# Decay levels of a gated recurrence on 32-column groups of TensorE, with two reorderings on VectorE

## The chip, the cores and the metric

The kernel runs on one core of a Trainium2 chip. The metric is the time of one execution on the device, in microseconds (us). Before the change it is 1099.34 us, the median of 3 runs (1099.16 to 1099.45). The profiled execution took 1100.05 us.

## The reference, cut to what matters

Two layers, each a chain of a feed-forward block, a mixer, a cross attention and another feed-forward block on 256 tokens of width 1024, all in float32. The change touches the recurrence inside the mixer and the softmax inside the cross attention.

```python
# hgrn2, per chunk of 64 tokens, 4 heads of 128 channels
b = jnp.cumsum(lb_, axis=2)                       # lb_ = log of the forget gate
diff = b[:, :, :, None, :] - b[:, :, None, :, :]
decay = jnp.exp(jnp.where(mask[:, :, None], diff, -jnp.inf))
attn = jnp.einsum('bhtd,bhsd,bhtsd->bhts', qb, kb, decay)
o = (jnp.einsum('bhts,bhsv->bhtv', attn, vb)
     + jnp.einsum('bhtd,bhdv->bhtv', qb * jnp.exp(b), state))
...
# cross_attn: 4 heads of 256 channels, 256 memory tokens
sc = jnp.einsum('bshd,bmhd->bhsm', q, k).astype(jnp.float32) * (CA_HEAD_DIM ** -0.5)
p = jax.nn.softmax(sc, axis=-1).astype(v.dtype)
o = jnp.einsum('bhsm,bmhd->bshd', p, v).reshape(bsz, s, D_MODEL)
```

## The kernel before

Every large matrix product is made of three products of split operands: a tile is cut into a high part in the f32r format (`split`, L60, a ScalarE copy at L61) and the rest (a VectorE subtraction at L62). Weights arrive through three `raw` buffers on the SyncE queue, are split into eight `whi` and eight `wlo` buffers, and are consumed by `product` (L106). So each of TensorE, VectorE and ScalarE has a steady load through the whole program.

The mixer (`mixer`, L586) computes the 256x256 decay-weighted products of `q` and `k` as a tree. Tokens are held as two blocks (`NT`) of 128, the second one reversed. The diagonal is one product `k` by `q` per head and block, with the identity picked out of it (L690, L691). Then come seven levels, `LEVELS = (1, 2, 4, 8, 16, 32, 64)`. In each, ScalarE gathers `kc`, the half blocks of `k` of that width (L701, `blocks`), TensorE multiplies `kc` by the other half blocks of `q` for all four heads (L713), VectorE scales `k` and `q` by the decay of a level (L729, L732), and it copies the entries of the level into `AT` under a mask (L739, `copy_predicated`, twice). At L713 all 128 columns of `kc` of a head stand on TensorE against 128 columns of `q`, although level `c` uses only the squares of width `c` beside the diagonal.

```python
for hh in range(HEADS):
    nc.tensor.matmul(
        o[:, hh], kc[:, hh, :],
        view(qf, hh * P + c, (other - c, 2), (2 * c, a), (1, c)),
        start=True, stop=True,
    )
```

TensorE's order in this part is the order of the code (`manual_schedule`, L671). Between the levels stand other products of the mixer (`products_of_others`, L710): one or two of them ahead of each level, so that VectorE and ScalarE can prepare the next level meanwhile. Behind the levels, `recurrence` (L761) multiplies `AT` by the values. The other engines' queues are ordered by a scheduler that goes by the order of the code and by what is ready.

The attention (`attention`, L854) takes four heads. `weights` (L876) makes the scores of a head, their maximum (L885), the exponentials (L892) and the division (L900), and sends the result through four transfers that deal it out (L904). `turned` (L907) transposes the dealt tile on VectorE (L909) and splits it. `mixed` (L921) multiplies it by the values. The scores of heads 2 and 3 are made while the second half of the values is made (`values`, L938 to L946), after heads 0 and 1 have been turned.

`small_parameters` (L214) loads parameters at the start, and its `later` (L252) works on them on VectorE; `later` is called in the first feed-forward block (L540 to L542).

Of the kernel before, what the change touches and what calls it, by code (L numbers as in the profile page):

```python
# [17 lines left out]
P = 128  # L18
# [4 lines left out]
NT = SEQ // P  # L23
NK = DM // P
HEADS = 4
# [4 lines left out]
LEVELS = (1, 2, 4, 8, 16, 32, 64)  # L30
# [16 lines left out]
def model(ctx: ExitStack, tc: tile.TileContext, t: dict, out: bass.AP):  # L47
    nc = tc.nc
# [5 lines left out]
    def acc(shape=(P, 2, SEQ), tag="acc"):  # L54
        return ps.tile(list(shape), F32, tag=tag, name=tag)


    loads, normed = [], []

    def split(hi, lo, src):  # L60
        nc.scalar.copy(hi, src)  # L61
        nc.vector.tensor_tensor(lo, src, hi.bitcast(F32), op=ALU.subtract)  # L62

# [115 lines left out]
    def load_memory(mp, behind):  # L179
# [25 lines left out]
    wpool = cst.tile([P, DEPTH, 2, P], F32, name="wpool")  # L205
    masks = cst.tile([P, 1024], U8, name="masks")[:, 0 : NT * len(LEVELS) * 64].rearrange(
        "p (b n c) -> p b n c", b=NT, c=64
    )
    nc.gpsimd.memset(nhalf, -0.5)
# [4 lines left out]
    def small_parameters(op):  # L214
# [12 lines left out]

        mf = op.tile([P, NT, len(LEVELS), 64], F32, name="mf", bufs=1)
        nc.gpsimd.memset(mf, 1.0)
        for b in range(NT):  # L230
            for n, c in enumerate(LEVELS):
# [9 lines left out]
        made = nc.gpsimd.tensor_copy(masks, mf)  # L241

# [128 lines left out]
    def ffn(l, name, n, pend=None, last=False, early=None):  # L371
        gate, up, down = (t[f"{name}_{x}"][l] for x in ("gate", "up", "down"))
        with tc.tile_pool(name="ffn", bufs=2, reuse_waits="tile") as fp:
# [155 lines left out]
            for c, (c0, ncol) in enumerate(chunks):  # L529
# [56 lines left out]
    def mixer(l, fill):  # L586
        w_in = t["w_in"][l]
        with tc.tile_pool(name="mix", bufs=1, reuse_waits="tile") as mp:
# [13 lines left out]
            v = mp.tile([P, NT, 512], F32, name="v")  # L602
            AT = mp.tile([P, NT, HEADS, P], F32, name="AT")
            AX_ = mp.tile([P, HEADS, P], F32, name="AX_")

# [79 lines left out]

            other = HEADS * P
            for b in range(NT):
                o = acc((P, HEADS, P), "dn")
                for hh in range(HEADS):
                    nc.tensor.matmul(o[:, hh, :], k[:, b, hh, :], q[:, b, hh, :], start=True, stop=True)  # L690
                nc.vector.tensor_tensor(  # L691
                    AT[:, b], o, idn[:, None, :].to_broadcast([P, HEADS, P]), op=ALU.mult
                )
            nc.vector.tensor_tensor(q, q, f, op=ALU.mult)
# [3 lines left out]
            def blocks(c):  # L698
# [6 lines left out]
                return kc  # L705

            kc = blocks(1)
            for n, c in enumerate(LEVELS):
                a = 64 // c
                products_of_others((1, 2, 1, 2, 1, 2, 2)[n])  # L710
                o = acc((P, HEADS, NT, 64), "dn")
                for hh in range(HEADS):
                    nc.tensor.matmul(  # L713
                        o[:, hh], kc[:, hh, :],
                        view(qf, hh * P + c, (other - c, 2), (2 * c, a), (1, c)),
                        start=True, stop=True,
                    )
                na, tb = HEADS * a, other // c
# [14 lines left out]
                if c < 64:  # L733
# [3 lines left out]
                    tot = nt[:, :]  # L737
                for b in range(NT):
                    nc.vector.copy_predicated(  # L739
                        AT[:, b].rearrange("p h (a w c) -> p h a w c", w=2, c=c)[:, :, :, 1 - b, :],  # L740
                        masks[:, b, n, :].rearrange("p (a c) -> p a c", c=c)[:, None].to_broadcast(
                            [P, HEADS, a, c]
                        ),
                        o[:, :, b].rearrange("p h (a c) -> p h a c", c=c),
                    )
            w_gate = load(w_in, 0, NK, 2304, 512)
# [14 lines left out]
            def recurrence(i):  # L761
# [6 lines left out]
                ss = sm.tile([P, HEADS], F32, tag="ss", name="ss")  # L768
                jk = mp.tile([P, P], F32, tag="jk", name="jk", bufs=2)
                for hh in range(HEADS):  # L770
# [83 lines left out]
    def attention(l, pend):  # L854
        scale = (DM // HEADS) ** -0.5
        with tc.tile_pool(name="att", bufs=1, reuse_waits="tile") as ap:
# [3 lines left out]
            vl = ap.tile([P, NT, DM], F32R, name="vl")  # L860
            pr = [None] * HEADS

# [13 lines left out]
            def weights(hh):  # L876
# [21 lines left out]
                for i in range(NT):  # L898
                    v = e.rearrange("p (q i j) -> p i q j", i=2, j=32)[:, i]
                    nc.vector.tensor_scalar_mul(v, v, s[:, i : i + 1])  # L900

                x = ap.tile([P, 4, 4, 32], F32, tag="dealt", name="dealt", bufs=2)
                for a in range(4):
# [17 lines left out]
            def mixed(hh, pT):  # L921
                o = acc()
                for d in range(2):
# [73 lines left out]
```

## Time and profile before

| | before |
|---|---|
| median of 3 runs | 1099.34 us |
| profiled execution | 1100.05 us |
| span in the profile | 1098.3 us |
| outside the span | 1.75 us |
| mean granted TensorE clock | 0.998 |

A line of a time-ordered view has the start and the length in us, the engine, the line of the code, the operation with what it writes and reads, and how many were merged ("x8"). A line of the groups has busy time and the mean duration in ns. One float32 matmul shows as two records, on PE and on PEld (the load of the columns that stand still). The length of a PE record is a latency, and records overlap, so what a matmul costs is read from the distance of two starts.

### The profile page before, as it was taken

The page shows a single profiled execution, that of the slowest core. Times are in us where ns is not written, and L with a number is a line of the kernel's source. Part 1 is how long each engine was busy: PE and PEld are TensorE (multiplying, and loading weights), DVE is VectorE, ACT ScalarE, POOL GpSimd, SP SyncE. Part 2 cuts the span into 40 slices and gives each one's busy share as a digit, 9 for nine tenths or more (in the row PEclk, how much of TensorE's full clock was granted, in tenths as well). Part 3 has the DMA queues.
Part 4 walks back from the last instruction along what each step waited for, and adds up shares of the span by engine and source line. Part 5 has one row for each costly group of instructions (what it writes and reads, how often), then busy time and mean ns, then how long its engine had stood idle before and what let it go on. Part 6 is the DMA issues. An engine that isn't in the chain of part 4 may idle for free.

```text
span 1098.3 us, 14694 instructions
## 1 busy us (share of the span) xinstructions
PE 1086.8 (99%) x5619; PEld 964.8 (88%) x5619; DVE 848.2 (77%) x1101; ACT 565.3 (51%) x767; POOL 61.2 (6%) x112
## 2 busy tenths in 40 slices
PE   9999999999999999999999999999999999999997
PEld 7888888999899888888888888899998988888886
DVE  6678678998989777666687655798989888766665
ACT  6466454665556455444455445456564654544450
POOL 9500000000000000000000000000000000000000
PEclk9999999999999999999999999999999999999999
DMA  9987664745485496766478676656446665876751
GB/s 319 303 278 234 212 215 160 255 156 173 160 265 190 134 301 216 231 216 222 154 264 265 219 217 211 224 171 213 161 131 229 237 201 166 259 243 213 215 169 39
DMA packets 122662, 231.79 MB, mean 211 GB/s; under 512 B 6304, under 2 KB 45504, under 8 KB 117472
## 3 DMA queue, kind: packets, MB, share of 16 engines
q1 hardware_dynamic: 120800, 228.48, 64.2%
q0 software_dynamic: 1216, 1.20, 0.4%
q10 hardware_dynamic: 576, 1.18, 0.3%
q8 instruction: 44, 0.72, 0.3%
q14 instruction: 26, 0.21, 0.1%
HBM read 216.15 MB, written 1.05 MB: 198 GB/s over the span
## 4 chain that ended last, share of the span: by engine, by line
PE 93%; DVE 4%; issue 1%; ACT 1%; DMA 0%; DVEq 0%; ACTq 0%
PE acc L106 61%; PE dn L106 28%; PE acc L170 1%; PE dn L713 1%; DVE square L909 1%; DVE wlo L62 1%; ACT e L892 0%; DVE qTl L62 0%; DMA h<-in_x_dram 0%; PE dn L767 0%; PE dn L690 0%; DVE mx L885 0%; DVE xT L62 0%; ACT L892 0%; DVE vl L62 0%
## 5 line engine op out<-in xcount | busy, mean ns | idle before, releaser
L62 DVE TENSOR_TENSOR wlo<-raw,whi 128x1024 fp32r<-128x1024 f32 (+1 forms) x396 | 473.8, 1213 | 177.9 <-ACT whi L61 168.6
L61 ACT CAST whi<-raw 128x1024 fp32r<-128x1024 f32 (+1 forms) x396 | 402.5, 1041 | 336.5 <-PE dn L106 139.9
L106 PE MATMUL acc<-whi,xT 128*128 128x512 f32 x1312 | 395.0, 379 | 0.0
L106 PEld LDWEIGHTS acc<-whi,xT 128*128 128x128 f32 x1312 | 247.8, 189 | 35.0
L106 PE MATMUL acc<-wlo,xT 128*128 128x512 f32 x656 | 248.6, 379 | 0.0
L106 PE MATMUL acc<-xT,whi 128*128 128x512 f32 x576 | 141.8, 382 | 0.0
L106 PEld LDWEIGHTS acc<-wlo,xT 128*128 128x128 f32 x656 | 124.0, 189 | 17.5
L106 PE MATMUL dn<-whi,ah 128*128 128x512 f32 x346 | 131.5, 380 | 0.0
L106 PE MATMUL dn<-wlo,ah 128*128 128x512 f32 x346 | 131.1, 379 | 0.0
L106 PE MATMUL dn<-whi,al 128*128 128x512 f32 x346 | 131.1, 379 | 0.0
L106 PEld LDWEIGHTS acc<-xT,whi 128*128 128x128 f32 x576 | 104.2, 190 | 11.2
L106 PE MATMUL dn<-whi,xT 128*128 128x512 f32 x288 | 89.0, 383 | 0.0
L106 PEld LDWEIGHTS acc<-xT,wlo 128*128 128x128 f32 x576 | 75.5, 191 | 3.9
L106 PE MATMUL acc<-xT,wlo 128*128 128x256 f32 x576 | 75.9, 275 | 0.0
L106 PEld LDWEIGHTS dn<-whi,al 128*128 128x128 f32 x346 | 65.4, 189 | 9.2
L106 PEld LDWEIGHTS dn<-wlo,ah 128*128 128x128 f32 x346 | 65.4, 189 | 9.2
L106 PEld LDWEIGHTS dn<-whi,ah 128*128 128x128 f32 x346 | 65.4, 189 | 9.2
L413 DVE STREAM_TRANSPOSE square<-dealt 128x512 f32<-128x512 f32 x40 | 63.3, 1650 | 1.8 <-DMA dealt<-sg 1.8
L322 POOL TENSOR_TENSOR rs<-rs,nhalf 128x1 f32<-128x1 f32 x16 | 14.9, 933 | 857.6 <-DVE rs L321 857.6
L106 PEld LDWEIGHTS dn<-whi,xT 128*128 128x128 f32 x288 | 54.5, 190 | 8.5 <-DVE xT L62 1.1
L106 PE MATMUL dn<-wlo,xT 128*128 128x512 f32 x144 | 54.8, 381 | 0.0
L315 DVE SCALAR_TENSOR_TENSOR h<-h,dn 128x512 f32<-128x512 f32 x31 | 21.2, 683 | 30.2 <-PE dn L106 30.2
(198 smaller groups left out, 996.7 us busy)
## 6 DMA issues: line engine op xcount, KB each, us to landing
raw<-in_ffn_up_dram SPq DMA_DIRECT2D x44, 1024.0 KB, 5.1
raw<-in_ffn_down_dram SPq DMA_DIRECT2D x44, 1024.0 KB, 5.2
raw<-in_ffn_gate_dram SPq DMA_DIRECT2D x42, 1024.0 KB, 5.1
raw<-in_w_in_dram SPq DMA_DIRECT2D x24, 1024.0 KB, 5.1
dealt<-sg SPq DMA_DIRECT2D x80, 128.0 KB, 3.2
raw<-in_ca_k_dram SPq DMA_DIRECT2D x8, 1024.0 KB, 5.0
raw<-in_w_out_dram SPq DMA_DIRECT2D x8, 1024.0 KB, 5.0
raw<-in_ca_v_dram SPq DMA_DIRECT2D x8, 1024.0 KB, 5.8
```

The costliest lines, as they stand in the source:

```text
L61: nc.scalar.copy(hi, src)
L62: nc.vector.tensor_tensor(lo, src, hi.bitcast(F32), op=ALU.subtract)
L106: nc.tensor.matmul(o, w, x, start=start, stop=stop)
L170: nc.tensor.transpose(pt[:, k, :], src[:, (4 * j + k) * P : (4 * j + k + 1) * P], unit)
L315: nc.vector.scalar_tensor_tensor(v, v, ALPHA / scale, sums(y[i][n]), op0=ALU.mult, op1=ALU.add)
L322: nc.gpsimd.tensor_tensor(rs, rs, nhalf[:, 0:1], op=ALU.pow)
L413: nc.vector.transpose(d.rearrange("p k (i b) -> p b k i", b=4), x[:, :, i, :].rearrange("p b (j k) -> p b k j", k=4))
L713: nc.tensor.matmul(o[:, hh], kc[:, hh, :], view(qf, hh * P + c, (other - c, 2), (2 * c, a), (1, c)), start=True, stop=True,)
L909: nc.vector.transpose(pt.rearrange("p m (i r b) -> p b (m i) r", i=2, b=4), pr[hh])
```

## The change

Diagonal and levels: for every head the 128 columns of `k` or `kc` are cut into four groups of 32, and each group is multiplied by the 32 columns of `q` that it needs (64 in level 64), into the 32 partitions of the output that belong to the group. The result is gathered in `square`, 32 wide, by masks 16 wide, in the levels below 32. In levels 32 and 64 ScalarE copies the result into `AT`, which GpSimd has set to zero; `square` is copied into `AT` at level 32.

```diff
-            for b in range(NT):
-                o = acc((P, HEADS, P), "dn")
                 for hh in range(HEADS):
-                    nc.tensor.matmul(o[:, hh, :], k[:, b, hh, :], q[:, b, hh, :], start=True, stop=True)
-                nc.vector.tensor_tensor(
-                    AT[:, b], o, idn[:, None, :].to_broadcast([P, HEADS, P]), op=ALU.mult
-                )
+                    for g in groups:
+                        nc.tensor.matmul(o[g, b, hh, :], k[:, b, hh, g], q[:, b, hh, g], start=True, stop=True)
+            nc.vector.tensor_tensor(
+                square, o, idc[:, None, None, :].to_broadcast([P, NT, HEADS, 32]), op=ALU.mult
+            )
...
-                o = acc((P, HEADS, NT, 64), "dn")
+                o = acc((P, HEADS, max(c, 32)), "dn")
                 for hh in range(HEADS):
-                    nc.tensor.matmul(
-                        o[:, hh], kc[:, hh, :],
-                        view(qf, hh * P + c, (other - c, 2), (2 * c, a), (1, c)),
-                        start=True, stop=True,
-                    )
+                    for j, g in enumerate(groups):
+                        if c < 32:
+                            x = view(qf, hh * P + 32 * j + c, (other - c, 2), (2 * c, 16 // c), (1, c))
+                        else:
+                            x = q[:, j * 32 // c % 2, hh, later(j, c)]
+                        nc.tensor.matmul(o[g, hh, :], kc[:, hh, g], x, start=True, stop=True)
...
+                else:
+                    if c == 32:
+                        for g in groups:
+                            nc.scalar.copy(AT[g, :, :, g], square[g])
+                    for at in range(0, P, c):
+                        g = slice(at, at + c)
+                        nc.scalar.copy(AT[g, at // c % 2, :, later(at // 32, c)], o[g])
```

Attention: the transfers of a head move out of `weights` into `deal`, and the scores and softmax of heads 2 and 3 are written ahead of the turning of heads 0 and 1.

```diff
-            query(1, lambda: (weights(0), weights(1)))
+            query(1, lambda: (weights(0), deal(0), weights(1), deal(1)))
...
-                    2: lambda: (pT.extend((turned(0), turned(1))), weights(2), weights(3)),
+                    2: lambda: (weights(2), weights(3), pT.extend((turned(0), turned(1))), deal(2), deal(3)),
```

Parameters: `later` is issued behind the latest subtraction of a split.

```diff
                 if c == 2:
-                    for f in rest:
-                        f()
+                    with tc.issue_after(lows[-1].ins):
+                        for f in rest:
+                            f()
```

On TensorE's queue, at the diagonal and the first level of a mixer, the order before and now (x4 counts matmuls merged into a row; the last two numbers are output partitions and moving columns):

```order
-L690 MATMUL dn<-q,k 128x128 x8
...
-L713 MATMUL dn<-q,kc 128x128 x4
+L701 MATMUL dn<-q,k 32x32 x32
...
+L736 MATMUL dn<-q,kc 32x32 x16
 L106 MATMUL acc<-xT,whi 128x512 x7
```

The products between stay as they were; each set of 4 or 8 matmuls has become one of 16 or 32 of a quarter of the width, and in the last level the moving width is 64.

On VectorE's queue in the first attention, before (mx_3227 is of head 2, mx_3255 of head 3, square_3202 of head 0, square_3208 of head 1):

```order
L909 STREAM_TRANSPOSE square_3202<-dealt_3095 128x4x128
L885 TENSOR_REDUCE mx_3227<-dn_3214 128x2
L885 TENSOR_REDUCE mx_3255<-dn_3242 128x2
L62 TENSOR_TENSOR pTl_3205<-square_3202,pTh_3204 128x512
L886 TENSOR_SCALAR mx_3227<-mx_3227 128x2
L886 TENSOR_SCALAR mx_3255<-mx_3255 128x2
L909 STREAM_TRANSPOSE square_3208<-dealt_3123 128x4x128
L897 RECIPROCAL sum_3231<-sum_3231 128x2
L900 TENSOR_SCALAR e_3230<-e_3230,sum_3231 128x8x32 x2
L62 TENSOR_TENSOR pTl_3211<-square_3208,pTh_3210 128x512
L897 RECIPROCAL sum_3259<-sum_3259 128x2
L900 TENSOR_SCALAR e_3258<-e_3258,sum_3259 128x8x32 x2
```

The same place in the changed kernel (mx_3326 is of head 2, mx_3349 of head 3, square_3359 of head 0, square_3365 of head 1):

```order
L913 TENSOR_REDUCE mx_3326<-dn_3313 128x2
L941 STREAM_TRANSPOSE square_3359<-dealt_3206 128x4x128
L914 TENSOR_SCALAR mx_3326<-mx_3326 128x2
L913 TENSOR_REDUCE mx_3349<-dn_3336 128x2
L62 TENSOR_TENSOR pTl_3362<-square_3359,pTh_3361 128x512
L914 TENSOR_SCALAR mx_3349<-mx_3349 128x2
L941 STREAM_TRANSPOSE square_3365<-dealt_3234 128x4x128
L925 RECIPROCAL sum_3330<-sum_3330 128x2
L928 TENSOR_SCALAR e_3329<-e_3329,sum_3330 128x8x32 x2
L925 RECIPROCAL sum_3353<-sum_3353 128x2
L928 TENSOR_SCALAR e_3352<-e_3352,sum_3353 128x8x32 x2
L62 TENSOR_TENSOR pTl_3368<-square_3365,pTh_3367 128x512
```

The maximum of head 2 moved ahead of the first transposition, and the division of head 3 ahead of the last split; the operations are the same.

More of the change, by code (lines that the diff above doesn't have):

```diff
@@ L240, in small_parameters @@
                 )
-        made = nc.gpsimd.tensor_copy(masks, mf)
+        for j in range(4):
+            g = slice(32 * j, 32 * j + 32)
+            nc.gpsimd.tensor_copy(idc[g], idn[g, g])
+            made = nc.gpsimd.tensor_copy(masks[g], mf[g, :, :, 16 * j : 16 * j + 16])
         cnt = op.tile([P, 2, PAD], F32, name="cnt", bufs=1)
@@ L737, in mixer @@
                     tot = nt[:, :]
-                for b in range(NT):
[L739 to L745, printed above, removed]
+                if c < 32:
+                    o = o.rearrange("p h (b t) -> p h b t", b=NT)
+                    for b in range(NT):
+                        nc.vector.copy_predicated(
+                            square[:, b].rearrange("p h (a w c) -> p h a w c", w=2, c=c)[:, :, :, 1 - b, :],
+                            masks[:, b, n, :].rearrange("p (a c) -> p a c", c=c)[:, None].to_broadcast(
+                                [P, HEADS, 16 // c, c]
+                            ),
+                            o[:, :, b].rearrange("p h (a c) -> p h a c", c=c),
+                        )
+                else:
[5 more added lines that the diff above has]
+                        nc.scalar.copy(AT[g, at // c % 2, :, later(at // 32, c)], o[g])
             w_gate = load(w_in, 0, NK, 2304, 512)
@@ L768, in recurrence @@
                 ss = sm.tile([P, HEADS], F32, tag="ss", name="ss")
[L769 removed]
+                jk = square[:, i].rearrange("p h t -> p (h t)")
                 for hh in range(HEADS):
```

27 lines of the change are left out of this document (19 added, 8 removed).

## The prediction

> **What bounds the kernel now.** I read the page's busy times first, then the chain of work that ended last, then the stretches that the change touches, then single records there. Busy time by engine, and the chain by engine:
>
> ```profile
> PE 1086.8 (99%) x5619; PEld 964.8 (88%) x5619; DVE 848.2 (77%) x1101; ACT 565.3 (51%) x767; POOL 61.2 (6%) x112
> ...
> PE 93%; DVE 4%; issue 1%; ACT 1%; DMA 0%; DVEq 0%; ACTq 0%
> ```
>
> TensorE (PE) is busy nearly throughout and is 93% of the chain: an edit pays where it takes work off TensorE, or where TensorE waits. The levels and the end of the attention, first layer; columns are the stretch, its length, busy us of PE, PEld, VectorE (DVE), ScalarE (ACT), GpSimd, then clock and DMA:
>
> ```profile
> 216.30:257.00 40.70, 40.70 (x265) 37.82 (x264) 39.81 (x73) 21.54 (x34) 0.00 (x0) 1.00 0.55 181
> 340.00:361.00 21.00, 20.07 (x116) 17.73 (x115) 19.69 (x29) 13.07 (x24) 0.00 (x0) 1.00 0.67 225
> ```
>
> In the levels TensorE never stops and VectorE is at 98%: a second limit just below. In the attention both have gaps. The chain there (start, length, what):
>
> ```profile
> 216.45 1.78 PE dn L690 x16
> 218.23 2.59 PE acc L106 x12
> 220.82 0.91 PE dn L713 x8
> 221.74 5.18 PE acc L106 x24
> ```
>
> So a layer spends 1.78 us on the diagonal and about 0.90 us on each of seven levels, all of it on the path: 8.1 us, 16.2 us in both layers. That is all that the first edit can touch on TensorE.
>
> **First edit: groups of 32 columns.** The float32 rows that it replaces, and a row of 256 columns in the other format (start, length, engine, line):
>
> ```profile
> L690 PE MATMUL dn<-q,k 128*128 128x128 f32 x32 | 3.9, 275 | 0.0
> L713 PE MATMUL dn<-q,kc 128*128 128x128 f32 x112 | 14.8, 275 | 0.0
> ...
> 327.15 0.28 PE L106 MATMUL dn<-kTl,qTh 128*128 128x256 f32 x1
> 327.26 0.28 PE L106 MATMUL dn<-kTh,qTl 128*128 128x256 f32 x1
> ```
>
> A float32 matmul of 128 moving columns is two records; eight records take 0.89 us, so one costs 111 ns. I found no record spaced closer than some 108 ns in this trace, so how TensorE takes a record of 32 columns is not shown. A level now has 16 matmuls, 32 records, each with a quarter of the moving columns and a quarter of the standing ones. Bounds per level from these rows:
> - Four groups fully side by side, time by moving columns: 32 records x 28 ns / 4 = 0.22 us.
> - One after another, time by moving columns: 32 x 28 = 0.89 us, as before.
> - One after another, each no cheaper than the closest spacing shown: 32 x 111 = 3.55 us.
>
> I take one half of the serial time, 0.45 us. It lies between the first two and is the case in which the two records of one matmul, which use the same columns of the array, follow each other while neighbouring matmuls, which use different groups, overlap. It is an estimate. Level 64 has 64 moving columns, so twice that: 0.89. The diagonal has 32 matmuls: 0.89 for 1.78.
>
> A change of shape costs something already:
>
> ```profile
> 221.49 0.47 PE L106 MATMUL acc<-whi,xT 128*128 128x512 f32 x1
> 221.79 0.38 PE L106 MATMUL acc<-wlo,xT 128*128 128x512 f32 x1
> 222.00 0.59 PE L106 MATMUL acc<-whi,xT 128*128 128x512 f32 x2
> ```
>
> Behind a level the first record lasts 0.30 us to the next start where the following lasts 0.21: 0.09 us. I allow another 0.10 us per set for the change of column width (bounds: 0, and 0.38, a whole record's latency here). In the Trainium skill, "TensorEngine Tiling (Array Packing)", section Key Properties, switching the tiling mode drains TensorE; no run here shows it yet, and by it the 0.10 is not zero.
>
> Sum per layer: six levels save 0.89 - 0.45 - 0.10 = 0.34 each, 2.04; level 64 loses 0.10; the diagonal saves 1.78 - 0.89 - 0.10 = 0.79. Together 2.73, **5.5 us in two layers**.
>
> Does something else become late? Ahead of level 1 VectorE must pick the diagonal and multiply `q`, and ahead of the fifth level it stands closest:
>
> ```profile
> 217.94 1.28 DVE L691 TENSOR_TENSOR AT<-dn,idn 128x512 f32<-128x512 f32 x2
> 219.14 1.22 DVE L694 TENSOR_TENSOR q<-q,f 128x1024 f32<-128x1024 f32 x1
> ...
> 238.94 0.67 DVE L732 TENSOR_TENSOR q<-q,tot 128x512 f32<-128x512 f32 x1
> 239.54 0.75 DVE L739 COPY_PREDICATED AT<-masks,dn 128x256 f32<-128x256 uint8 x2
> 239.93 1.05 PE L713 MATMUL dn<-q,kc 128*128 128x128 f32 x8
> ```
>
> `q` is ready at 219.14 + 1.22 = 220.36 and TensorE comes at about 220.66: 0.3 us. At the fifth level, 239.61 against 239.93: 0.3 us again. TensorE cannot gain more than VectorE does. What VectorE gains:
>
> ```profile
> L739 DVE COPY_PREDICATED AT<-masks,dn 128x256 f32<-128x256 uint8 x28 | 12.9, 530 | 0.0
> L691 DVE TENSOR_TENSOR AT<-dn,idn 128x512 f32<-128x512 f32 x4 | 2.6, 682 | 0.0
> L127 DVE TENSOR_TENSOR f<-acc,f 128x256 f32<-128x256 f32 x8 | 3.3, 418 | 0.0
> L886 DVE TENSOR_SCALAR mx<-mx 128x2 f32<-128x2 f32 x8 | 1.1, 162 | 0.1
> L126 ACT COPY q<-acc 128x256 f32<-128x256 f32 x8 | 3.0, 370 | 4.7 <-PE acc L106 4.5
> ```
>
> The diagonal goes from two of 0.68 to one of the kind of 0.42: 0.9 us. Of 14 masked copies of 128x256 ten remain, of 128x64; between 0.16 (a tiny one) and 0.46 (now, 12.9 us by 28) I take 0.2, nearer to the tiny one, since they are a quarter as long. That frees 14 x 0.46 - 10 x 0.2 = 4.4 us, so 5.3 us a layer, and 2.9 of it (0.9 and four levels' 0.5) ahead of the fifth level. TensorE's own gain there is 0.79 + 4 x 0.34 = 2.15. The forecast passes; fully side by side it would not quite. ScalarE gets ten small copies, none over the 0.37 of the 128x256 row, at most 3.7 us onto 21.54 of 40.70: covered. GpSimd zeroes `AT` while idle (0.00 in the row above), long before it is read. If that cover went, TensorE would wait as long as the copy is late, 0.4 us at level 64.
>
> **Second edit: softmax of heads 2 and 3 earlier.** TensorE and VectorE at the end of the attention:
>
> ```profile
> 345.38 0.69 DVE L62 TENSOR_TENSOR pTl<-square,pTh 128x512 fp32r<-128x512 f32 x1
> 346.30 0.17 DVE L897 RECIPROCAL sum<-sum 128x2 f32<-128x2 f32 x1 [0.23 <-ACT e L892]
> 346.50 0.62 DVE L900 TENSOR_SCALAR e<-e,sum 128x256 f32<-128x256 f32 x2
> 347.03 0.68 DVE L62 TENSOR_TENSOR vl<-acc,vh 128x512 fp32r<-128x512 f32 x1
> ...
> 352.33 1.55 DVE L909 STREAM_TRANSPOSE square<-dealt 128x512 f32<-128x512 f32 x1
> ...
> 355.86 0.27 PE L106 MATMUL acc<-qTh,vh 128*128 128x256 f32 x1
> 356.18 0.38 PE L106 MATMUL acc<-qTl,vh 128*128 128x256 f32 x1
> ...
> 357.40 0.28 PE L106 MATMUL acc<-qTh,vl 128*128 128x256 f32 x1
> 358.21 0.38 PE L106 MATMUL acc<-qTh,vh 128*128 128x256 f32 x1 [0.54 <-ACT qTh L61]
> 358.94 0.38 PE L106 MATMUL acc<-qTl,vh 128*128 128x256 f32 x1 [0.35 <-DVE qTl L62]
> ```
>
> Between these starts 0.11 us would do: TensorE loses 0.21, 0.70 and 0.62, about 1.5 us a layer, waiting for heads 2 and 3. But VectorE works almost without a break from 346.50 to the transposition at 352.33, and the orders of the two kernels agree from `vl` on. So the edit can give only what it takes out ahead of `vl`: the 0.23 us at 346.30 and some 0.2 us of smaller gaps, in which VectorE waited for ScalarE's exponentials. Bounds: 0, and 1.5. I take 0.4 a layer, **0.8 us**, near the first since the row of the wait is 0.23. The last split of head 1 moves from 345.38 to about 346.0, and `mixed(1)` begins at 348.05: covered by 1.4 us. SyncE issues the same transfers in the same order; those of heads 2 and 3 are not what VectorE waits for at 352.33.
>
> **Third edit: parameters.** At the start of the program:
>
> ```profile
> 8.97 0.37 DVE L257 TENSOR_SCALAR cnt<-cnt,wcol 128x16 f32<-128x16 f32 x2
> 9.37 0.35 DVE L258 RECIPROCAL invc<-cnt 128x32 f32<-128x32 f32 x1
> 10.21 0.69 DVE L62 TENSOR_TENSOR xT<-acc,xT 128x512 fp32r<-128x512 f32 x1 [0.48 <-ACT xT L61]
> ```
>
> Behind the removed operations VectorE still waits 0.48 us for ScalarE, so taking them out gives nothing. Their new place is in the first feed-forward block, far ahead of the mixer at 216. Cost 0; if they delayed a split there, some 12 operations of 0.16 us, 2 us.
>
> **Sum.** 1100.05 - 5.5 - 0.8 = 1093.8 for an execution like the profiled one (its span is 1098.3, with 1.75 outside). The median of the runs shown is 0.7 lower, so 1093.0.
>
> **Rivals.** A measurement of this kernel tells about 0.2%, 2.2 us, from no change.
> 1. *Fully side by side.* Six levels 0.22 + 0.10 save 0.57 each; level 64 saves 0.35; the diagonal 1.2, which is also what VectorE allows there (0.9 and the 0.3 in hand). That is 5.0 a layer. By the fifth level TensorE would be 1.2 + 4 x 0.57 = 3.5 ahead and VectorE 2.9 + 0.3 = 3.2, so 0.3 is lost: 4.7, in two layers 9.4, with the attention 10.2: 1089.2. For it: the groups share neither columns nor outputs. Against: VectorE at 98%. In the Trainium skill, "TensorE: Matmul & The Clock Gate", Measured speedup vs the span model, three column tiles of 512 columns run 2.38 times as fast; no row here shows 32 columns.
> 2. *Three quarters of the serial time.* Six levels save 0.12, level 64 loses 0.54, the diagonal saves 0.35: 0.5 a layer, 1.0; with the attention 1.9: 1097.4, no change that can be told.
> 3. *A fixed price per record: slower.* It decides from 28 ns a record, at which even serial groups are even, less the switch. Each record that the trace spaces at 111 ns comes with a load on PEld, so two entries per 111 ns, 56 ns each, is shown to be possible. At 56 ns: six levels 1.79 + 0.10, each 1.0 more; level 64 the same; the diagonal 1.9 more: 8.9 a layer, 17.8, less 0.8: 1116.3. At 28 ns and level 64 at 1.79 us it is 1.7 a layer more: 1101.9, about the border. In the same page of the Trainium skill, section Wait — 56ns, not 53.3ns?, a small matmul costs 62 ns where the sequencer decodes in microcode, and 25 ns at least otherwise; by 62 in place of 56 the 576 records would add 3.5 us to this rival.
> 4. *The edit is not felt in the attention*, or wholly: 0.8 less or 2.2 more of gain, inside the ranges.
>
> **How the numbers follow.** Forecast (about half) 0.40; fully side by side 0.20; three quarters 0.17; slower 0.23. Faster 0.60, same 0.17, slower 0.23. Alone, the forecast has 1091 to 1096. The range goes down to 1087.5, below the first rival by the rest of the attention's wait, and up to 1106, some 30 ns a record; it leaves out about 0.05 below and 0.13 above.
>
> **What would show it.** The distance from the first record of a level to the first L106 record behind it: about 0.55 us by the forecast, 0.32 side by side, 1.9 with a fixed price. The distance at the diagonal: 1.0. Waits of TensorE for VectorE in the levels: none. The gaps of TensorE ahead of the last `mixed`: 1.1 us in place of 1.5. I would be wrong if records of 32 columns have a floor of their own, or if VectorE, not TensorE, holds the levels.

## The result, and the profile after

The changed kernel took 1093.30 us (median of 4 runs, 1093.20 to 1093.65), the kernel before 1099.39 us beside it (4 runs, 1099.16 to 1099.49). The ratio is 0.9945, with a 95% interval of 0.9928 to 0.9963: 6.1 us less. The profiled execution took 1093.2 us; its span is 1091.4 us, 6.9 less than before.

First the page's busy times. The line has more records on PE (6051, before 5619) and fewer busy us:

```profile
PE 1079.9 (99%) x6051; PEld 953.4 (87%) x6051; DVE 836.9 (77%) x1091; ACT 571.7 (52%) x787; POOL 60.8 (6%) x113
...
PE 93%; DVE 4%; ACT 1%; issue 1%; DMA 0%; DVEq 0%; ACTq 0%
```

TensorE is still busy throughout and still 93% of the chain: what bounds the kernel has not changed, there is less of it. The stretch of the levels that the prediction looked at, taken between the same places of the program (length; busy us of PE, PEld, VectorE, ScalarE, GpSimd; granted clock; DMA):

```profile
215.54:253.26 37.72, 37.72 (x481) 32.89 (x481) 35.34 (x70) 24.69 (x44) 0.00 (x0) 1.00 0.58 197
```

It was 40.70 us long before and is 37.72 now. VectorE has 35.34 us of work in it (before 39.81), ScalarE 24.69 (before 21.54). TensorE's records in order of time there (start, length, line, operation, how many), at the diagonal, at level 1 and at level 64:

```profile
215.21 0.38 PE L106 MATMUL acc<-whi,xT 128*128 128x512 f32 x1
215.52 0.76 PE L701 MATMUL dn<-q,k 128*32 128x32 f32 x64
216.21 0.48 PE L106 MATMUL acc<-whi,xT 128*128 128x512 f32 x1
216.53 0.38 PE L106 MATMUL acc<-wlo,xT 128*128 128x512 f32 x1
...
218.69 0.38 PE L106 MATMUL acc<-whi,xT 128*128 128x512 f32 x1
219.00 0.46 PE L736 MATMUL dn<-q,kc 128*32 128x32 f32 x32
219.39 0.48 PE L106 MATMUL acc<-whi,xT 128*128 128x512 f32 x1
219.71 0.38 PE L106 MATMUL acc<-wlo,xT 128*128 128x512 f32 x1
...
248.66 0.65 PE L736 MATMUL dn<-q,kc 128*32 128x64 f32 x32
249.25 1.78 PE L106 MATMUL acc<-xT,whi 128*128 128x512 f32 x7
```

Of the kernel before, the record ahead of the diagonal, those ahead of and at level 1, and the one behind the last level's products:

```profile
216.07 0.38 PE L106 MATMUL acc<-whi,xT 128*128 128x512 f32 x1
...
220.44 0.38 PE L106 MATMUL acc<-whi,xT 128*128 128x512 f32 x1
220.66 1.08 PE L713 MATMUL dn<-q,kc 128*128 128x128 f32 x8
...
255.71 1.05 PE L756 MATMUL dn<-q,k 128*128 128x128 f32 x8
```

The reader is to take distances of starts, not the lengths. A level: 219.00 to 219.39, 0.39 us; before, 220.66 to the 221.49 of the prediction's row, 0.83. Ahead of it the last L106 record takes 0.31 us to the next start, where it took 0.22 (220.44 to 220.66); behind it the first one takes 0.32 (before 0.30). So a level with its edges takes 0.31 + 0.39 + 0.32 = 1.02 us, and took 0.22 + 0.83 + 0.30 = 1.35. In the same way the diagonal takes 1.32 us (215.21 to 216.53) and took 2.22 (216.07 to 218.29), with 0.69 us between its first record and the next product, and level 64 takes 0.59 us in the middle and took 0.81 (252.20 to 253.01). From the last L106 record ahead of the diagonal to the first record behind level 64's products it is 36.76 us (215.21 to 251.97), before 39.64 (216.07 to 255.71): **2.88 us a layer, 5.8 us in both** (the second layer's stretch is shorter by as much).

In the attention, TensorE's records where it waits for heads 2 and 3 (in brackets the wait and its releaser):

```profile
352.12 0.27 PE L106 MATMUL acc<-qTh,vh 128*128 128x256 f32 x1
352.33 0.38 PE L106 MATMUL acc<-qTl,vh 128*128 128x256 f32 x1
...
353.55 0.28 PE L106 MATMUL acc<-qTh,vl 128*128 128x256 f32 x1
354.37 0.38 PE L106 MATMUL acc<-qTh,vh 128*128 128x256 f32 x1 [0.54 <-ACT qTh L61]
355.09 0.38 PE L106 MATMUL acc<-qTl,vh 128*128 128x256 f32 x1 [0.35 <-DVE qTl L62]
```

The gaps beyond 0.11 us are 0.10, 0.71 and 0.61, together 1.42 us a layer; they were 1.53. That is 0.2 us in both layers. The remaining 0.9 us by which the profiled executions differ lies in the first 20 us, and most of it is no gain. The profiled execution of before took 0.7 us more than its median. And in the kernel with the softmax edit alone (below), which leaves the start as it was, TensorE's first `acc<-whi,xT` record stands at 19.15 us, against 19.69 before and 18.83 in the changed kernel: over half of that difference comes without an edit.

### The profile page after: what moved, and what is told of

It reads as the page before. It is cut to its first block, busy times and chain, and to the rows that moved or that the text cites. A ratio compares the mean times of both kernels' runs of the same rounds, so it can differ in the third digit from the quotient of the medians.

```text
span 1091.4 us, 15575 instructions
## 1 busy us (share of the span) xinstructions
PE 1079.9 (99%) x6051; PEld 953.4 (87%) x6051; DVE 836.9 (77%) x1091; ACT 571.7 (52%) x787; POOL 60.8 (6%) x113
## 4 chain that ended last, share of the span: by engine, by line
PE 93%; DVE 4%; ACT 1%; issue 1%; DMA 0%; DVEq 0%; ACTq 0%
PE acc L106 62%; PE dn L106 28%; PE acc L170 1%; DVE wlo L62 1%; DVE square L941 1%; PE dn L736 1%; DVE qTl L62 0%; PE dn L795 0%; DMA h<-in_x_dram 0%; ACT e L920 0%; DVE mx L913 0%; ACT L920 0%; DVE e L928 0%; DVE vl L62 0%; ACT whi L61 0%
## 5 line engine op out<-in xcount | busy, mean ns | idle before, releaser
L106 PE MATMUL acc<-whi,xT 128*128 128x512 f32 x1312 | 394.9, 380 | 0.0
L106 PEld LDWEIGHTS acc<-whi,xT 128*128 128x128 f32 x1312 | 247.8, 189 | 35.3
L106 PE MATMUL acc<-wlo,xT 128*128 128x512 f32 x656 | 248.6, 379 | 0.0
L106 PE MATMUL acc<-xT,whi 128*128 128x512 f32 x576 | 142.1, 382 | 0.0
L106 PEld LDWEIGHTS acc<-wlo,xT 128*128 128x128 f32 x656 | 124.0, 189 | 17.3
L106 PE MATMUL dn<-whi,ah 128*128 128x512 f32 x346 | 131.5, 380 | 0.0
L106 PE MATMUL dn<-wlo,ah 128*128 128x512 f32 x346 | 131.1, 379 | 0.0
L106 PE MATMUL dn<-whi,al 128*128 128x512 f32 x346 | 131.1, 379 | 0.0
L106 PEld LDWEIGHTS acc<-xT,whi 128*128 128x128 f32 x576 | 104.1, 190 | 11.8
L106 PE MATMUL dn<-whi,xT 128*128 128x512 f32 x288 | 88.6, 382 | 0.1
L106 PEld LDWEIGHTS acc<-xT,wlo 128*128 128x128 f32 x576 | 75.5, 191 | 3.9
L106 PE MATMUL acc<-xT,wlo 128*128 128x256 f32 x576 | 75.9, 275 | 0.0
L106 PEld LDWEIGHTS dn<-whi,al 128*128 128x128 f32 x346 | 65.4, 189 | 9.3
L106 PEld LDWEIGHTS dn<-wlo,ah 128*128 128x128 f32 x346 | 65.4, 189 | 9.2
L106 PEld LDWEIGHTS dn<-whi,ah 128*128 128x128 f32 x346 | 65.4, 189 | 9.1
L106 PEld LDWEIGHTS dn<-whi,xT 128*128 128x128 f32 x288 | 54.2, 189 | 8.7 <-DVE xT L62 1.0
L106 PE MATMUL dn<-wlo,xT 128*128 128x512 f32 x144 | 54.8, 380 | 0.3 <-DVE wlo L62 0.3
```

The costliest lines, as they stand in the source:

```text
L106: nc.tensor.matmul(o, w, x, start=start, stop=stop)
```

## The experiments

**One edit at a time.** Three kernels have one edit each; the other two are taken back.

The levels on groups alone:

```diff
-                    with tc.issue_after(lows[-1].ins):
-                        for f in rest:
-                            f()
+                    for f in rest:
+                        f()
...
-                    2: lambda: (weights(2), weights(3), pT.extend((turned(0), turned(1))), deal(2), deal(3)),
+                    2: lambda: (pT.extend((turned(0), turned(1))), weights(2), weights(3)),
```

> The kernel before with the first edit alone (groups of 32 columns). Theory A, from the traces of before and after: nearly all of the gain is TensorE's own time in the levels, 2.88 us a layer between the last product ahead of the diagonal and the product behind the levels, so 5.8 us: 1099.4 - 5.8 = 1093.6, and the distances in the levels are those of the changed kernel (0.39 us from the first record of a level to the next L106 record). Theory B, the prediction: 5.5 us from the levels, 0.8 from the softmax: 1093.9. Theory C, that the 0.86 us by which the changed kernel's profile is ahead in its first 20 us belong to the parameters: then this kernel is at 1094.2 or above.

Measured: 1102.61 us, ratio 1.0027 (1.0017 to 1.0038). The edit that was to bring nearly all of the gain is, alone, slower than the kernel before, and of the times given beforehand only the open end of theory C reaches there; its reason, 0.86 us for the parameters, does not. Its levels look as after the whole change. What differs is the start. VectorE, GpSimd and TensorE there, each in order of time:

```profile
7.99 0.68 DVE L62 TENSOR_TENSOR wlo<-raw,whi 128x512 fp32r<-128x512 f32 x1
16.31 0.37 DVE L262 TENSOR_SCALAR cnt<-cnt,wcol 128x16 f32<-128x16 f32 x2 [7.64 <-POOL cnt L252]
16.59 0.68 DVE L62 TENSOR_TENSOR xT<-acc,xT 128x512 fp32r<-128x512 f32 x1
```
```profile
16.12 0.16 POOL L252 IOTA cnt<- 128x32 f32 x1
```
```profile
17.33 1.22 PE L106 MATMUL dn<-whi,xT 128*128 128x512 f32 x2 [6.93 <-DVE xT L62]
```

VectorE has nothing running from 8.67 (7.99 + 0.68) to 16.31: at the head of its queue stands the smaller of the counts and the widths (`cnt<-cnt,wcol`), and GpSimd makes the counts only at 16.12. Behind that small operation waits the split of `xT` (16.59), and for that one TensorE stands 6.93 us. In the kernel before, the same operation ran at 8.97 without a wait, since GpSimd had counted long before:

```profile
7.28 0.16 POOL L247 IOTA cnt<- 128x32 f32 x1
```

And TensorE does not come back at full speed. The four us behind its wait, in the run with the levels alone (columns as above; the granted clock is the third number from the end):

```profile
17.30:21.30 4.00, 3.97 (x9) 3.16 (x10) 4.00 (x7) 0.00 (x0) 3.96 (x8) 0.50 0.27 65
```

At a clock of 0.50 these four us do the work of two, so by this estimate the wait costs 6.9 + 2.0 us. (The Trainium skill, "TensorE: Matmul & The Clock Gate", What's actually happening, has TensorE fall back to half its clock after some 3.4 us without work; the row agrees.)

The first edit has GpSimd make the masks differently, and in the order that results the fills of `wcol` and the counting stand behind most of the mask work.

The softmax alone (the second diff of the change), and the parameters alone (the third):

> The kernel before with the second edit alone (softmax of heads 2 and 3 ahead of the turning of 0 and 1). Theory B, the prediction: VectorE is 0.4 us earlier a layer from the split of the values on, TensorE's gaps at the last two heads fall from 1.5 to 1.1 us, 1098.6. Theory A: VectorE's wait for the exponentials is replaced by a wait for ScalarE's cast ahead of the split of head 0, the gaps go from 1.53 to 1.42 us, 0.1 a layer: 1099.2, not told from the kernel before.

> The kernel before with the third edit alone (parameters' part later). Theory A and B: nothing, 1099.4. Theory C: 0.7 to 0.9 us less, 1098.6, with TensorE's long run of products starting near 9.9 us instead of 10.6 in the profile.

Measured: 1099.31 us, ratio 0.9998 (0.9989 to 1.0007), and 1099.26 us, ratio 0.9998 (0.9989 to 1.0007). Neither is worth anything in the kernel before.

**Is that wait the whole loss?** Two kernels take it away in two ways. One has the first and the third edit, without the second:

> The change without its second edit: the levels on groups, and the parameters' part of VectorE queued later; softmax as before. The first edit alone had taken 1102.6 us, and in its trace VectorE stood from 8.67 to 16.31 us with the two operations on the counts at the head of its queue, waiting for GpSimd. Theory W (that wait is the whole loss, and queueing those operations later takes it away): 1093.3 us and, for the softmax that is undone, 0.2 more, so 1093.3 to 1093.8; no wait of VectorE for the counts in the first 20 us; TensorE's long run of products ends near 19 us, not 28. Theory S (the loss of the first edit has its cause elsewhere, and the softmax is what mends it): about 1102. Theory H (both mend it half): about 1098.

The other has the first edit alone, with GpSimd's counting put back ahead of the masks:

```diff
+        cnt = op.tile([P, 2, PAD], F32, name="cnt", bufs=1)
+        wcol = op.tile([P, 2], F32, name="wcol", bufs=1)
+        ...
+        nc.gpsimd.iota(cnt, pattern=[[0, 2], [1, PAD]], base=1, channel_multiplier=0, ...)
         narrow = [c for c in LEVELS if c < 32]
...
-        cnt = op.tile([P, 2, PAD], F32, name="cnt", bufs=1)
```

> The first edit alone, as in the run that took 1102.6 us, with one thing moved: on GpSimd the fills of the windows' widths and the counting run ahead of the work on the masks, as they stood in the kernel before; the parameters' part of VectorE stays where it was. Theory W (VectorE waits for the counts, which the first edit's code put behind the masks): the counts are there at about 7.5 us, VectorE does not stand, 1093.3 to 1094.3 us. Theory M (the mask work on GpSimd itself, or its transfers, holds the start): 1101 to 1103 us as before.

Measured: 1093.63 us (ratio 0.9949, 0.9937 to 0.9962) and 1094.12 us (0.9954, 0.9942 to 0.9967). Both times are as theory W says. In the second, VectorE and GpSimd at the start, and TensorE's only wait in the levels (line waiting, line waited for, us in total, times, longest):

```profile
6.49 0.16 POOL L233 IOTA cnt<- 128x32 f32 x1
```
```profile
8.84 0.37 DVE L262 TENSOR_SCALAR cnt<-cnt,wcol 128x16 f32<-128x16 f32 x2
```
```profile
PE dn L735 <- DVE q L704: 0.5, 1, 0.5
```

The counts are there at 6.49 + 0.16, VectorE takes them at 8.84 and does not stand. Where the other 0.5 us between the two medians lies is not shown. The one wait in the last line, at level 1 of the second layer, is of that size, but this execution took 1095.32 us, 1.2 above its median. VectorE's margin there is thin: in the changed kernel `q` is ready at 757.18 us and TensorE comes at 757.55. So the third edit is worth 9.0 us (1102.6 against 1093.6) together with the first, the wait's 6.9 + 2.0, and nothing without it.

The run with edits one and three also shows the second edit from the other side: 1093.63 with it taken back, 1093.30 with it. In its trace the first gap of the attention's end is

```profile
352.65 0.27 PE L106 MATMUL acc<-qTh,vh 128*128 128x256 f32 x1
352.97 0.38 PE L106 MATMUL acc<-qTl,vh 128*128 128x256 f32 x1
```

0.32 less 0.11, 0.21 us, as before the change; the two others are the same as after. The softmax gives 0.1 us a layer.

**Why a level takes 0.39 us.** The first kernel has the same matmuls, in an order in which four in a row go to the same group:

```diff
-                for hh in range(HEADS):
-                    for j, g in enumerate(groups):
+                for j, g in enumerate(groups):
+                    for hh in range(HEADS):
```

> The changed kernel with the loops over heads and groups exchanged, so that four matmuls in a row stand on the same group of 32 columns and the next four on the next; the same records and results. If neighbours run side by side because their groups differ: most of it goes, records come every 27 ns (a quarter of 107), a level takes 0.09 + 32 x 0.027 = 0.95 us in place of 0.39, level 64 1.8 in place of 0.59, the diagonal 1.8 in place of 0.69: 11 us slower in all, 1104.5. If a record has a price of its own of some 10 ns whatever its group: no change, 1093.3. If a matmul of the next group is taken ahead: between.

The second takes all heads on groups 0 and 1 in turn, then all heads on 2 and 3:

```diff
+                for two in (0, 2):
                     for hh in range(HEADS):
-                    for j, g in enumerate(groups):
+                        for j in (two, two + 1):
```

> The changed kernel with the matmuls of a set in another order: all heads on groups 0 and 1 in turn, then all heads on groups 2 and 3. With four matmuls in a row on the same group the time was 1101.6 us and a level lasted 0.84 us in place of 0.39. Theory N (a matmul overlaps only with its next neighbour, where that is on another group; two groups in turn are enough): 1093.3 us, a level 0.39 us. Theory F (all four groups run at once, and each group is busy in turn): two groups give about half the gain, a level 0.6 us, 1097.4 us.

Measured: 1101.62 us (ratio 1.002, 1.0011 to 1.0029) with one group, 1095.92 us (0.997, 0.9958 to 0.9981) with two. TensorE at level 1, with one group and then with two:

```profile
219.86 0.90 PE L736 MATMUL dn<-q,kc 128*32 128x32 f32 x32
220.70 0.48 PE L106 MATMUL acc<-whi,xT 128*128 128x512 f32 x1
```
```profile
219.23 0.61 PE L739 MATMUL dn<-q,kc 128*32 128x32 f32 x32
219.76 0.48 PE L106 MATMUL acc<-whi,xT 128*128 128x512 f32 x1
```

The same 32 records take 0.84 us with one group, 0.53 with two in turn, 0.39 with four. Level 64 takes 1.32, 0.83 and 0.59, the diagonal 1.45, 0.87 and 0.69. One group came as the first reading had it, that neighbours run side by side because their groups differ, though 2.9 us below its 1104.5. The numbers of a level are 0.24 + 0.60 / n for n groups in turn (0.84, 0.54, 0.39), those of level 64 are 0.34 + 0.98 / n (1.32, 0.83, 0.59); the diagonal does not fit such a line (it would give 0.58 for four). Two groups are not enough, so theory N falls; more groups go on helping, as theory F has it, though F had put two groups too high (0.6 us, 1097.4). So order matters as much as shape: with one group at a time the changed kernel is 2.3 us slower than the kernel before.

The third kernel keeps the order and asks for the price of a set. In the four levels with two products ahead of them, one of these goes into the midst of the level:

```diff
-                products_of_others((1, 2, 1, 2, 1, 2, 2)[n])
+                products_of_others(1)
...
                 for hh in range(HEADS):
+                    if hh == 2 and (1, 2, 1, 2, 1, 2, 2)[n] == 2:
+                        products_of_others(1)
```

> The changed kernel, with the same matmuls; in the four levels that have two products of others ahead of them, one of the two is put in the midst of the level, between heads 1 and 2. So TensorE goes from whole columns to groups and back eight times more in the two layers. Theory X (each such set has a price of its own: about 0.10 us ahead of it, 0.09 in it and 0.11 behind it, as read off the trace): 8 x 0.3 = 2.4 us more, 1095.7 us. Theory R (the price is per record, whatever stands around it): 1093.3 us, no change. In the trace a half set would last 0.09 + 16 x 0.0094 = 0.24 us to the next product by X, 0.20 by R.

Measured: 1096.00 us (ratio 0.997, 0.9959 to 0.9981), 2.7 us more for eight sets, 0.34 us each. One of the half sets at level 2, and one at level 64:

```profile
221.96 0.38 PE L106 MATMUL acc<-whi,xT 128*128 128x512 f32 x1
222.27 0.33 PE L738 MATMUL dn<-q,kc 128*32 128x32 f32 x16
222.53 0.48 PE L106 MATMUL acc<-whi,xT 128*128 128x512 f32 x1
222.85 0.38 PE L106 MATMUL acc<-wlo,xT 128*128 128x512 f32 x1
...
247.13 0.43 PE L738 MATMUL dn<-q,kc 128*32 128x64 f32 x16
247.49 1.78 PE L106 MATMUL acc<-xT,whi 128*128 128x512 f32 x7
```

Half a set takes 0.26 us and a whole one 0.39, so 16 records add 0.13 and a set has 0.13 us that no record accounts for. With 0.10 ahead of it (0.31 against 0.21) and 0.11 behind it (0.32 against 0.21) that makes 0.34, the price that the time shows. (0.09 of the piece behind it stood behind a set before, too.) Theory X holds, and is 0.04 us low. A record itself costs 0.13 / 16 = 8 ns. With 64 moving columns (the last two rows) half a set takes 0.36 us and a whole one 0.59, so there a record costs 0.23 / 16 = 14 ns, and the set has the same 0.13 us besides.

The fourth has as many matmuls of as many moving columns, but all 128 columns of `kc` (at the diagonal, of `k`) stand; the four results of a head overwrite one another, so the decay-weighted products are left wrong:

```diff
-                        nc.tensor.matmul(o[g, hh, :], kc[:, hh, g], x, start=True, stop=True)
+                        nc.tensor.matmul(o[:, hh, :], kc[:, hh, :], x, start=True, stop=True)
```

> The changed kernel with the same count of matmuls in each set and the same 32 (at level 64, 64) moving columns, but on all 128 columns of the array instead of a group of 32; the results of a head's four matmuls overwrite one another, so the block part of the gates' attention is left wrong, and this only measures. Theory G (groups of columns bring the overlap, and the change of the column width brings the price): a level lasts as long as before, 32 records x 28 ns less what its start overlaps = 0.82 us, 0.21 us ahead of it; level 64 1.7 us; about 1101 us in all. Theory S (short records bring the price, whatever their width): 0.82 us too, but 0.31 us ahead of a set, 1102.5 us. Theory L (short records, not groups, bring the gain): a level 0.39 us, 1093.3 us.

Measured: 1171.44 us (ratio 1.0655, 1.0641 to 1.0670). TensorE at level 1 and at level 64 of the first layer, then four stretches (columns as above):

```profile
230.16 0.38 PE L106 MATMUL acc<-whi,xT 128*128 128x512 f32 x1
230.37 3.65 PE L736 MATMUL dn<-q,kc 128*128 128x32 f32 x32
233.86 0.46 PE L106 MATMUL acc<-whi,xT 128*128 128x512 f32 x1
```
```profile
284.62 3.68 PE L736 MATMUL dn<-q,kc 128*128 128x64 f32 x32
288.12 1.76 PE L106 MATMUL acc<-xT,whi 128*128 128x512 f32 x7
```
```profile
160.00:216.00 56.00, 56.00 (x317) 50.61 (x316) 47.55 (x73) 31.34 (x44) 3.18 (x7) 1.00 0.58 195
216.00:226.00 10.00, 10.00 (x63) 10.00 (x63) 1.51 (x3) 0.00 (x0) 0.00 (x0) 0.68 0.59 211
226.00:260.00 34.00, 34.00 (x217) 31.48 (x217) 19.25 (x36) 12.34 (x18) 0.00 (x0) 0.90 0.26 93
230.00:234.00 4.00, 4.00 (x36) 3.95 (x35) 0.00 (x0) 0.58 (x1) 0.00 (x0) 1.00 0.00 0
```

None of the theories had this. A record with 128 standing columns takes 3.49 / 32 = 109 ns whether 32 or 64 columns move (level 64: 3.50 / 32), close to the 111 ns of the kernel before, where 128 move. The clock does not explain it: around level 1 it is 1.00 (the last row). With 32 standing columns of one group and 32 moving ones it is 0.84 / 32 = 26 ns, a quarter. So with 128 standing columns a record does not get cheaper when fewer columns move. With 32 standing ones the moving columns do count: at level 64 one group after another takes 1.32 / 32 = 41 ns a record, and four groups in turn 14 ns in place of 8. The prediction's 28 ns "by moving columns" came out near 26 in a change that cuts both to a quarter. One thing is not separated here: the four matmuls of a head also write the same place one after another. On the other point theory G holds: ahead of the level the product takes 0.21 us, not 0.31, so the 0.10 us ahead of a set belongs to the change of the column width. The total is no measure of the records alone, since the granted clock fell, to 0.68 around the diagonal, where it was 1.00 just before.

**Versions that might beat both.** The diagonal and level 1 as one set, so one set fewer in a layer:

```diff
+            products_of_others(1)
+            nc.scalar.copy(AT, q)
...
-                        nc.tensor.matmul(o[g, b, hh, :], k[:, b, hh, g], q[:, b, hh, g], start=True, stop=True)
+                        nc.tensor.matmul(o[g, b, hh, :], k[:, b, hh, g], AT[:, b, hh, g], start=True, stop=True)
...
+            nc.gpsimd.memset(AT, 0.0)
```

> The changed kernel with the diagonal and level 1 as one set: ScalarE copies the raw queries into the attention's tile ahead of it, the diagonal reads them there, VectorE's multiplication of the queries goes ahead, and the product of others that stood between the two sets goes ahead of both. The same matmuls, one change to groups and back fewer in a layer. Theory X (each set has a price of some 0.34 us, as eight more sets cost 2.7 us): 0.7 us less, 1092.6 us. Rival V (VectorE and ScalarE, which now both work ahead of the set, come late by up to the multiplication's 1.2 us): up to 1.7 us more, 1095.0 us.

A second buffer for the turning of head 3, and in the same kernel the last slab of weights is loaded and split behind the last turning:

```diff
+                if hh == 3:
+                    pt = ap.tile([P, NT, SEQ], F32R, tag="pTh", name="square", bufs=2).bitcast(F32)
+                else:
+                    pt = sm.tile([P, 2, SEQ], F32, tag="sums", name="square", bufs=1)
...
+                    with tc.issue_after(turns[-1].ins) if a == 6 else nullcontext():
+                        w = load(t["ca_o"][l], a, 2, 0, DM)
```

> The changed kernel with a second buffer for the turning at the end of the attention: head 3 is turned into a buffer of its own and need not wait for the split of head 2 to read the first; the splits of the last slab of weights there are issued behind the last turning. The gaps of TensorE there were 0.10 + 0.71 + 0.61 us a layer and the softmax edit left them. Theory B (the one buffer, on which the turning of head 3 waits, holds TensorE): most of the 1.4 us a layer goes, 1090.6 us; 1091.5 if half. Rival D (the transfers of heads 2 and 3, which come last, hold it): 1093.3 us.

And both:

> The changed kernel with the two edits of the last two runs together, one set fewer in a layer and the second buffer for the turning. If each does what theory X and theory B say, and they don't touch each other: 1089.9 us; otherwise the sum of what the two runs measured.

Measured: 1092.80 us (ratio 0.9941, 0.9928 to 0.9953), 1091.89 us (0.9932, 0.9919 to 0.9944) and 1091.22 us (0.9926, 0.9912 to 0.9939; runs from 1090.89 to 1091.45). One set fewer gave 0.5 of the 0.7 us by the medians. The trace has it more sharply: from the start of the product ahead of the diagonal to the record behind level 64's products it is 38.81 us (212.89 to 251.70), in the changed kernel 39.13 (212.84 to 251.97), so 0.32 us a layer, near the 0.34 of a set. The second buffer with the later splits gave 1.4 of the 2.7 us; TensorE there, and what VectorE does meanwhile:

```profile
352.22 0.27 PE L106 MATMUL acc<-qTh,vh 128*128 128x256 f32 x1
352.33 0.28 PE L106 MATMUL acc<-qTl,vh 128*128 128x256 f32 x1
...
357.55 0.70 PE L106 MATMUL dn<-whi,xT 128*128 128x512 f32 x2 [0.76 <-DVE xT L62]
```
```profile
353.41 3.49 DVE L62 TENSOR_TENSOR wlo<-raw,whi 128x1024 fp32r<-128x1024 f32 x3
```

The three gaps are gone (352.22 to 352.33 is 0.11, and no wait stands in the rest of it). But the three splits, 3.49 us together, which now come late, stand ahead of the split of `xT`, and TensorE waits 0.76 us for that: half the gain turned into a new wait. Rival D falls, since the transfers are the same and the gaps went. Theory B fits, but the run changes the buffer and the place of the splits at once, so what the buffer does alone is not shown. The last kernel gives about the sum of the two (2.1 us, against 0.5 + 1.4). It is the fastest of the study, 2.1 us below the changed one; the two were not run side by side, but the kernel before took 1099.31 us beside the one and 1099.39 beside the other.

## Why the prediction was right, and where it was not

- **Levels, 5.5 us.** The trace shows 5.8, and the run with edits one and three 5.6. The terms: a level was to save 0.34 and saved 0.31 to 0.33, the diagonal 0.79 and saved 0.90, level 64 was to lose 0.10 and gained 0.11. What was to be seen, a distance of 0.55 us, came out as 0.39, in part since 0.10 us of the price of the switch lies ahead of the set: with that it is 0.49.
- **The mechanism behind the 0.45.** The prediction took half of the serial time, because the two records of a matmul share a group and would follow each other while neighbours overlap. By that, two groups in turn would do as well as four; they don't (0.53 against 0.39 us). The runs show instead records that run nearly fully side by side, as the first rival has it (8 ns each, where its 28 / 4 is 7; 14 ns at level 64, where its 56 / 4 is 14), and a price per set that is larger than the 0.10 allowed: 0.34, of which 0.09 was there before. Two sizes were off, in opposite directions, by about the same: 0.45 + 0.10 foretold, and 0.39 + 0.10 + 0.02 found against a level that really cost 0.83 and not 0.89. That the two nearly cancel, so that 5.5 us came so close, is luck.
- **The switch and the drain.** The rule that the prediction quoted from the Trainium skill, "TensorEngine Tiling (Array Packing)", Key Properties, that a change of tiling mode drains TensorE, speaks for a price at each change, and the runs show one: 0.34 us a set, of which the 0.10 ahead of it is gone when the width stays at 128. That it is a drain they don't show. What they do show is that the load of a set's first columns no longer runs ahead. In the kernel before it starts 0.19 us ahead of the level's first record (220.47 against 220.66), in the changed kernel with it (219.00), after 0.33 us without a load:

```profile
220.47 1.06 PEld L713 LDWEIGHTS dn<-q,kc 128*128 128x128 f32 x8
```
```profile
219.00 0.35 PEld L736 LDWEIGHTS dn<-q,kc 128*32 128x32 f32 x32 [0.33 <-issue]
```

- **The third rival** (a fixed price per record) did not come: 8 ns. But the 111 ns that the prediction reads for a record came again in the whole-width run, 109 ns, with a quarter of the moving columns: where all 128 columns stand there is such a price. The Trainium skill, "TensorE: Matmul & The Clock Gate", LDWEIGHTS, has a load's time follow the number of columns and not of rows; 109 ns for 128 and 26 for 32 agree, and the 41 ns at 64 moving columns is not the load's alone.
- **VectorE as the next limit.** It was to have 5.3 us less work a layer and has 4.5 less (39.81 to 35.34), against the 2.98 by which the stretch became shorter. TensorE has no wait in the levels; in the traces of two other kernels (the counting put back, the second buffer) it has one of 0.5 us, at level 1 of the second layer. ScalarE took 3.2 us more, inside the 3.7.
- **Softmax, 0.8 us.** Mis-sized: 0.2 by the trace, 0.0 alone. The prediction let the 0.23 us wait ahead of `vl` go. It went, and another came in its place. VectorE, first layer:

```profile
339.09 0.69 DVE L62 TENSOR_TENSOR pTl<-square,pTh 128x512 fp32r<-128x512 f32 x1 [0.22 <-ACT pTh L61]
```

VectorE now waits 0.22 us for ScalarE's half of the first turning. And what held TensorE was further on, in the one buffer of the turning, as the run with a second buffer and later splits suggests: both kernels have that one buffer, so an order ahead of it could give little.
- **Parameters, 0.** Right for this edit in the kernel before (1099.26 us), wrong for the changed kernel, in which it is worth 9.0 us. The step that failed is "taking them out gives nothing": it read VectorE's wait in the trace of before, and took the three edits as terms of a sum. The first edit moves GpSimd's counting from 7.28 to 16.12 us, by which the parameters' operations would hold VectorE for 7.6 us; the third takes them out of the way (in the changed kernel GpSimd counts at 18.87 us, and VectorE takes the counts at 90.2). The prediction looked at GpSimd only where it zeroes `AT`, not at the start. The sum came out because both edits were made together: the first alone is 3.3 us slower than the kernel before.
- **Smaller slips.** The range's lower end is 1087.0 by the prediction's own terms (1089.2 less 2.2), not 1087.5, and its 1106 is some 36 ns a record by the third rival's sum (1101.9 at 28 ns, 512 records), not 30. And starts closer than 108 ns do stand in the trace of before, where one kind of product follows another: level 64 takes 0.81 us, of which seven steps of 111 ns are 0.78, so the next product starts some 0.03 us behind its last record. None of this enters the 1093.0.

## What to carry to other kernels

Small matmuls on column groups pay when neighbours in the queue go to different groups, and when they stand together in long sets: count the sets (0.34 us each here), the standing and the moving columns of each record, and how many groups take turns. Parts of a change are not terms of a sum: when one part adds or moves work on an engine that looks idle, look at what waits for it in the new order of every queue, above all for a small operation at the head of an in-order queue. Where a wait goes away, look for the resource behind it (here, it seems, a single buffer) before pricing the gain.

## What the runs showed of the hardware that was not expected

- A float32 record with 128 standing columns takes 109 ns, with 32 or with 64 moving columns; with 32 standing columns, one group after another, 26 ns, the set's own price included; with four groups in turn each further record adds 8 ns. With 64 moving columns on 32 standing ones it is 41 and 14 ns.
- Going from whole columns to groups and back costs 0.34 us a set, in three pieces: 0.10 ahead, 0.13 in it, 0.11 behind (0.09 of the last stands behind a float32 set of whole columns, too). The load of the set's first columns does not run ahead under the product before it.
- In the run with records of 128 standing and 32 moving columns the granted clock fell to 0.68 around the diagonal and was 0.90 in the mean of the 34 us behind it (1.00 at level 1), without a wait of TensorE there, where the stretches of before and after that are shown here have 1.00.
